# The output projection of a hybrid decoder layer by Strassen's seven products, with the combinations of weights and of the second half's input kept at the source's place in each engine's order

## The chip, the cores and the metric

The kernel runs on one core of one Trainium2 chip. Its time is the device time of one execution in microseconds; a run's time is the median of several executions where more than one is given. The engines are TensorE (PE, with its weight loads apart as PEld), VectorE (DVE), ScalarE (ACT), GpSimd (POOL) and SyncE, whose queue (SP) issues every DMA of this kernel.

## What is computed

One step of a Hymba-style layer: an RMS norm of the input, one input projection to all heads' queries, keys, values and gates, three kinds of recurrent heads (6 mLSTM heads "A", 6 gated-delta-rule heads "B", 4 HGRN2 heads "C", each 128 wide), a norm and a gate for each head, the output projection, the residual, a final norm. The width is 2048; there are 1024 prompt tokens, 16 meta tokens ahead of them, and 8 x 8 sample tokens. All is fp32. The end of it, which the change is about, is in the reference

```python
h = _rmsnorm(x, norm_w)
proj = jnp.einsum('bld,de->ble', h, w_in)
...
hcat = jnp.concatenate([ha, hb, hc], axis=2)
hcat = hcat * lax.rsqrt(jnp.mean(hcat * hcat, axis=-1, keepdims=True) + EPS)
y = hcat.reshape(bsz, L, MIX) * out_norm_w.astype(f32) * jax.nn.silu(z.astype(f32))
out = jnp.einsum('ble,ed->bld', y.astype(x.dtype), w_out)
return x + out, ...
...
y_prompt = _rmsnorm(xp[:, N_META:], final_norm_w)
```

so `out` is a product of 1024 x 2048 (and 64 x 2048 for the samples) by 2048 x 2048.

## The kernel before

The prompt is worked off in two halves of 512 tokens; the first half also holds the meta and the sample tokens. Every fp32 product is made of three fp32r products: each operand is split into a part `hi` and a rest `lo`, and hi·hi, hi·lo and lo·hi are added up. Weights come as pieces of 128x512: `feed_raw` loads one (tile `wraw`, four buffers), `feed_split` lets ACT cast it to `whi` and VectorE subtract to get `wlo` (four buffers each), and `feed_ahead` keeps the splits three pieces and the loads seven pieces ahead of the piece that TensorE is at. There are 720 pieces, 144 of them for the output projection.

For each half the heads are projected in the order of `ORDER` (C0 B0 A0 B1 A1 C1 B2 A2, then B3 A3 C2 B4 A4 B5 A5 C3); in the second half a piece is 12 matmuls of 128x512 (matmuls into `acc`). Between the matmuls the program weaves the heads' own work, as generators in four queues: `scan` (the recurrence), `fin` (`finish`: the head's norm, a turn through DRAM, the gate, the split into hi and lo, the store to `y_dram`), `post`, and `bg` (background: the preparation of the second half's input `prep_B`, norm states). A model clock (`Clock`) sets when a step is due, `Weave.pump` places due steps, and `drain` places all that is left of a stream. Behind that a scheduler may still move instructions within each engine's order, as far as their dependencies and its own estimate of their times allow. Each engine, and SP's queue, then works its instructions off in order.

A B head's scan (`gdn_scan`) solves a triangular system: `pkk` and `pqk` (matmuls of keys with keys and with queries) are scaled into `Ball`, its diagonal blocks make a turn through DRAM (`db`, `Bb`), VectorE substitutes in thirty small steps (`Yt`, `Yc`), transposes into `X`, and TensorE goes on with `pz` and `pyy`.

The output projection (1754 on) runs over `OUT_UNITS`: for the first half four groups of 512 columns with the half's four prompt tiles and the sample tile, for the second half the same without samples, the last group split in two. A unit takes 16 pieces (`o_raw`, one for each head of 128 rows), each with three matmuls for each prompt tile and two for the sample tile, into `oacc`. Then the tile of x is loaded and added, squared and summed, multiplied by the final norm's weights on POOL, and `final_norm` scales and stores the rows (tiles `res`, `oscr`, `fr`).

## Time and profile before

| | |
|---|---|
| median of three runs | 2505.61 us (2505.42 to 2511.15) |
| the profiled execution | 2506.0 us |
| its span | 2504.3 us, mean granted TensorE clock 0.990 |
| PE busy | 2442.1 us (98%) |
| VectorE, ACT, POOL busy | 1425.5, 991.2, 554.8 us |
| DMA | 350.82 MB, mean 140 GB/s |
| first and last output matmul | 2102.1 and 2493.5 us |

The span is the time between the first and the last instruction of the profiled execution. Busy times are sums over instructions, and since matmuls are pipelined and their ends modelled, a busy PE is not PE at its peak. L137 is the line of the helper that issues every engine instruction, so groups are told apart by their tiles.

### The profile page before, as it was taken

The numbers are of one execution on the slowest core, as the hardware profiler recorded it, in microseconds if no ns is written. First come the engines' busy times: TensorE is split into PE (matmuls) and PEld (weight loads), VectorE is DVE, ScalarE is ACT, GpSimd is POOL, SyncE is SP. The second block draws the span as 40 slices with busy tenths as digits, with TensorE's granted clock in tenths as the row PEclk, the third lists the DMA queues.
The fourth block names the chain that finished last, engine by engine and source line by source line (L and its number), as shares of the span: only waits on it lengthen the run. The fifth ranks groups of instructions, "written<-read, shape, count | busy, mean of one in ns | idle before, by whom it ended". The sixth has DMA issues, their size and how long they took to land.

```text
span 2504.3 us, 43941 instructions
## 1 busy us (share of the span) xinstructions
PE 2442.1 (98%) x16032; PEld 2184.5 (87%) x16032; DVE 1425.5 (57%) x3080; ACT 991.2 (40%) x2430; POOL 554.8 (22%) x743
## 2 busy tenths in 40 slices
PE   6999999999999999999999999999999999999998
PEld 5898999999999999999787888888888888888886
DVE  7775655765656655556864556554654545323435
ACT  5643434443435333333642434333443334222324
POOL 5331212420313312113320113110320102211201
PEclk9999999999999999999999999999999999999999
DMA  5656665655645454447554455454554558636735
GB/s 129 152 140 147 147 146 133 162 131 130 158 99 138 99 131 118 118 119 203 132 132 115 120 123 136 122 130 101 138 127 114 129 123 257 183 84 200 254 97 185
DMA packets 681045, 350.82 MB, mean 140 GB/s; under 512 B 260004, under 2 KB 622076, under 8 KB 680828
## 3 DMA queue, kind: packets, MB, share of 16 engines
q1 hardware_dynamic: 680828, 348.01, 54.3%
q8 instruction: 126, 2.06, 0.4%
q14 instruction: 91, 0.75, 0.1%
HBM read 285.71 MB, written 62.19 MB: 139 GB/s over the span
## 4 chain that ended last, share of the span: by engine, by line
PE 80%; issue 5%; DVE 5%; DMA 4%; ACT 2%; POOL 2%; SPq 1%; POOLq 0%; DVEq 0%; ACTq 0%
PE acc L137 59%; PE oacc L137 9%; PE pa L137 1%; DVE wlo L137 1%; PE po L137 1%; PE nd L137 1%; PE pz L137 1%; PE pyy L137 1%; DMA wraw<-in_w_in_dram 1%; POOL res L137 1%; PE pu L137 1%; DMA px<-in_x_prompt_dram 1%; ACT whi L137 1%; PE poh L137 1%; PE pw L137 1%
## 5 line engine op out<-in xcount | busy, mean ns | idle before, releaser
L137 DVE TENSOR_TENSOR wlo<-wraw,whi 128x512 fp32r<-128x512 f32 x720 | 525.6, 734 | 569.6 <-ACT whi L137 552.1
L137 PE MATMUL acc<-hA,whi 128*128 128x288 f32 (+1 forms) x4544 | 826.2, 304 | 11.3 <-ACT whi L137 6.4
L137 ACT CAST whi<-wraw 128x512 fp32r<-128x512 f32 x720 | 441.9, 618 | 929.1 <-PE acc L137 641.2
L137 PE MATMUL acc<-hB,whi 128*128 128x512 f32 x2272 | 722.2, 400 | 4.3 <-ACT whi L137 2.1
L137 PEld LDWEIGHTS acc<-hA,whi 128*128 128x128 f32 x4544 | 679.6, 191 | 18.2 <-ACT whi L137 8.1
L137 PE MATMUL acc<-hA,wlo 128*128 128x288 f32 x2240 | 489.7, 299 | 1.6 <-DVE wlo L137 1.6
L137 PEld LDWEIGHTS acc<-hB,whi 128*128 128x128 f32 x2272 | 413.6, 189 | 86.2 <-ACT whi L137 2.7
L137 PE MATMUL acc<-hB,wlo 128*128 128x512 f32 x1120 | 441.1, 394 | 2.6 <-DVE wlo L137 2.6
L137 PEld LDWEIGHTS acc<-hA,wlo 128*128 128x128 f32 x2240 | 367.7, 190 | 2.7 <-DVE wlo L137 2.6
L137 PE MATMUL oacc<-whi,y 128*128 128x512 f32 x1088 | 343.4, 390 | 1.1 <-ACT whi L137 1.1
L137 PEld LDWEIGHTS acc<-hB,wlo 128*128 128x128 f32 x1120 | 211.0, 188 | 52.0 <-DVE wlo L137 6.8
L137 PEld LDWEIGHTS oacc<-whi,y 128*128 128x128 f32 x1088 | 204.2, 188 | 44.5 <-ACT whi L137 2.4
L137 PE MATMUL oacc<-wlo,y 128*128 128x512 f32 x576 | 224.8, 390 | 1.2 <-DVE wlo L137 1.2
L137 PEld LDWEIGHTS oacc<-wlo,y 128*128 128x128 f32 x576 | 108.1, 188 | 25.2 <-DVE wlo L137 3.1
L137 POOL TENSOR_TENSOR res<-res,fnw 128x512 f32<-128x512 f32 (+1 forms) x34 | 54.3, 1627 | 255.4 <-ACT oscr L137 255.4
L137 POOL TENSOR_TENSOR y<-y,zs 128x592 fp32r<-128x592 f32 (+1 forms) x32 | 46.0, 1437 | 171.4 <-ACT zs L137 106.7
L137 POOL TENSOR_TENSOR qd<-qT,emb 128x512 f32<-128x512 f32 x12 | 17.7, 1479 | 230.3 <-PE po L137 230.3
L137 DVE TENSOR_TENSOR Yt<-Yc,Bb 128x60 f32<-128x60 f32 (+8 forms) x180 | 37.6, 209 | 43.9 <-DMA Bb<-db 39.0
L137 POOL TENSOR_TENSOR hr<-hr,halfneg 128x4 f32<-128x4 f32 (+1 forms) x48 | 44.1, 919 | 61.1 <-DVE hr L137 58.4
L137 POOL TENSOR_TENSOR nrm<-nrm,halfneg 128x10 f32<-128x10 f32 x12 | 23.5, 1960 | 138.9 <-DVE nrm L137 138.9
L137 POOL TENSOR_TENSOR X<-Ex,hk 128x256 f32<-128x256 f32 (+1 forms) x40 | 39.1, 978 | 63.2 <-PE pa L137 41.8
L137 ACT ACTIVATE Wt<-pw,nrm 128x128 f32<-128x128 f32 (+1 forms) x54 | 19.8, 367 | 78.1 <-PE pw L137 78.1
(416 smaller groups left out, 2766.7 us busy)
## 6 DMA issues: line engine op xcount, KB each, us to landing
wraw<-in_w_in_dram SPq DMA_DIRECT2D x564, 256.0 KB
wraw<-in_w_out_dram SPq DMA_DIRECT2D x144, 256.0 KB
y<-y SPq DMA_DIRECT2D x16, 576.0 KB
px<-in_x_prompt_dram SPq DMA_DIRECT2D x32, 256.0 KB
yd<-y SPq DMA_DIRECT2D x128, 64.0 KB
out_dram<-sst SPq DMA_DIRECT2D x16, 512.0 KB
s<-yd SPq DMA_DIRECT2D x32, 256.0 KB
y<-zs SPq DMA_DIRECT2D x32, 256.0 KB
```

Source lines behind the costliest of these rows:

```text
L137: return f(out, *a, **k)
```

## The change

The product is cut into 2 x 2 x 2 blocks: token halves, heads in two sets (`K1`, the first eight of `ORDER`, and `K2`, the other eight), and column halves. With A the gated heads' output and B the weights, seven block products take the place of eight. They use combinations of A's blocks, S1 to S4, and of B's, T1 to T4; A12, A21 and so on are never multiplied alone except where the scheme has them. The products run in seven phases over two buffers of y in turn; a phase has two parts `j` of 512 columns. The sample tokens' product isn't changed in its number of matmuls, and is done beside the phases that use the plain weights.

Beside the seven products it changes:

- `combine_weights`, a background stream of the second half: 16 times four loads of 128x512 weights, four POOL subtractions, four stores (`w_comb`). The 64 products' pieces then load from there (`c_raw`). The output projection has 152 pieces.
- `finish` of the first half also stores y whole (`y_whole`) and its POOL subtraction waits for that store, since it writes over y. In the second half a head of K1 makes S3 of y and the first half's y (one POOL step), a head of K2 makes S1, S2, S4 and A22 (three POOL steps); each combination is cast by ACT, subtracted by VectorE (by POOL before) and stored in two parts (`y_comb`).
- `load_y` loads the combinations for a phase and drains those finishes first whose results it needs.
- Partial sums (`t1`, `q`) stay in SBUF; ACT, VectorE and POOL move and add them between phases. x is loaded and added late.
- `prep_B` and `combine_weights` are pinned: their instructions keep the source's place in each engine's order (`tc.keep_in_program_order`), DMAs included.

The core of the diff:

```diff
+K1, K2 = HEADS[:NH // 2], HEADS[NH // 2:]
+LAST_UNITS = [(0, range(4)), (1, range(2)), (1, range(2, 4))]
...
+    def DMA(*a):
+        ins = nc.sync.dma_start(*a)
+        if ck.pin:
+            ck.pin(ins)
+        return ins
...
+    for j in range(2):
+        pieces += out_pieces(j, K1, j)
+    for j in range(2):
+        for a, b in zip(out_pieces(j, K2, j), out_pieces(j, K1, j + 2)):
+            pieces += [a, b]
+    for j in range(2):
+        for kk, b in enumerate(out_pieces(j, K2, j + 2)):
+            pieces += [(c_raw, "T2", j, kk), b]
+    for j in range(2):
+        pieces += [(c_raw, "T1", j, kk) for kk in range(NK // 2)]
+    for j in range(2):
+        pieces += out_pieces(j, K2, j + 2)
+    for j in range(2):
+        pieces += [(c_raw, "T3", j, kk) for kk in range(NK // 2)]
+    for j, _ in LAST_UNITS:
+        pieces += [(c_raw, "T4", j, kk) for kk in range(NK // 2)]
...
     def finish(half, head, outs, ssq, scale, zs):
...
+        if not half.first:
+            DMA(ya, y_whole[0][K1[kk]])
+            if not upper:
+                DMA(yb, y_whole[1][kk])
+                DMA(yc, y_whole[0][head])
...
+        if half.first:
+            S.copy(yhi[:, 0:W], y[:, 0:W])
+            ck.last += 1.0
+            yield
+            DMA(y_whole[0][head], y[:, 0:HALF])
+            ck.last = ck.t["T"] + 2.0
+            yield
+            G.tensor_tensor(ylo[:, 0:W], y[:, 0:W], yhi[:, 0:W], op=ALU.subtract)
...
+        def parts(src, hi, name):
+            S.copy(hi, src)
+            ck.sync()
+            V.tensor_tensor(src.bitcast(F32R), src, hi, op=ALU.subtract)
+            d = y_comb[name][kk].bitcast(F32)
...
+        G.tensor_tensor(yb, yb, y, op=ALU.add)
+        yield
+        yield from parts(y, yhi, "A22")
+        G.tensor_tensor(ya, yb, ya, op=ALU.subtract)
+        yield
+        yield from parts(yb, spare, "S1")
+        G.tensor_tensor(yc, yc, ya, op=ALU.subtract)
+        yield
+        yield from parts(ya, yhi, "S2")
+        yield
+        yield from parts(yc, spare, "S4")
...
+    def load_y(u, n, src):
+        if isinstance(src, str):
+            weave.drain(*(fins[1, h] for kk in (2 * n, 2 * n + 1) for h in (K1[kk], K2[kk])))
...
+    def combine_weights():
+        for j in range(2):
+            for kk in range(NK // 2):
+                b11, b12, b21 = (sp.tile([P, 512], F32, tag="px", name="px", bufs=3) for _ in range(3))
+                b22 = sp.tile([P, 512], F32, tag="pxs", name="pxs", bufs=1)
+                for t, heads, cg in ((b11, K1, j), (b12, K1, j + 2), (b22, K2, j + 2), (b21, K2, j)):
+                    DMA(t, i["w_out"][0, P * heads[kk]:P * (heads[kk] + 1), 512 * cg:512 * (cg + 1)])
+                for dst, a, b in ((b11, b12, b11), (b12, b22, b12), (b22, b22, b11), (b21, b21, b22)):
+                    ck.last = ck.t["T"] + 7.0
+                    yield
+                    G.tensor_tensor(dst, a, b, op=ALU.subtract)
+                ck.last = ck.t["T"] + 4.0
+                yield
+                for n, t in (("T1", b11), ("T3", b12), ("T2", b22), ("T4", b21)):
+                    DMA(w_comb[n][NK // 2 * j + kk], t)
...
+            weave.add("bg", combine_weights(), pin=tc.keep_in_program_order)
...
-                weave.add("bg", prep_B())
+                weave.add("bg", prep_B(), pin=tc.keep_in_program_order)
...
+    def phase(u, j, accs, tiles, own=None, other=None, each=None):
+        for kk in range(NK // 2):
+            whi, wlo = next_piece()
+            for n in tiles:
+                yh, yl = (y_block(u, kk, n, part) for part in (0, 1))
+                T.matmul(accs[n], yh, whi, start=kk == 0, stop=False)
+                T.matmul(accs[n], yh, wlo, start=False, stop=False)
+                T.matmul(accs[n], yl, whi, start=False, stop=kk == NK // 2 - 1)
...
+    for j, tiles in LAST_UNITS:
+        accs = banks(tiles)
+        phase(0, j, accs, tiles)
+        weave.drain_queue("post")
+        late = tiles[-1] == NC - 1 and j == 1
```

How the instructions move is seen at three places. First TensorE's order at head B4 of the second half, before (`acc` is the projection, `hB` the normed input, the rest the solver's tiles named above):

```order
L137 MATMUL pkk<-Ck 128x128 x4
L137 MATMUL acc<-hB_14743,whi 128x512
L137 MATMUL acc<-hB_14744,whi 128x512
L137 MATMUL acc<-hB_14743,wlo 128x512
...
L137 MATMUL pqk<-Cq,Ck 128x128 x4
...
L137 MATMUL pvb<-ident,Cv 128x128 x4
...
L137 MATMUL pz<-X_21883,Ball 32x32 x16
```

and in the change:

```order
L138 MATMUL acc<-hB_14984,wlo 128x512
L138 MATMUL pkk<-Ck 128x128 x4
L138 MATMUL pqk<-Cq,Ck 128x128 x4
L138 MATMUL pvb<-ident,Cv 128x128 x4
L138 MATMUL pz<-X_22217,Ball 32x32 x16
L138 MATMUL acc<-hB_14767,whi 128x512
L138 MATMUL acc<-hB_14768,whi 128x512
```

Before, 9, 6 and 78 projection matmuls stand in the three gaps; now there are none between `pkk` and `pz`.

Second POOL's order where the second half begins (`px` and `pxs` are the weights being combined; `sst`, `state_C` and `hr` belong to the scan and the finish of the first half's last head):

```order
L138 TENSOR_TENSOR pxs<-pxs,px 128x512
L138 TENSOR_TENSOR px<-px,pxs 128x512
L138 TENSOR_TENSOR sst<-sst,eP 128x8x128
L138 COPY state_C_772<-s_15301 128x128
L138 TENSOR_TENSOR hr<-hr,halfneg 80x1
L138 TENSOR_TENSOR hr<-hr,halfneg 128x4
L138 TENSOR_TENSOR px<-px 128x512
L138 TENSOR_TENSOR px<-pxs,px 128x512
```

The rows on `px` and `pxs` are new; they stand ahead of and between the steps of that scan.

Third ACT's order in the first half, where before the squares of the second half's input (`pxs<-px`) stand among the gate scan's steps:

```order
L137 ACTIVATE Lr<-Lr 128x592
L137 CAST whi<-wraw 128x512
L137 ACTIVATE pxs,bss<-px 128x512
L137 ACTIVATE gt_970<-pre 128x592
L137 ACTIVATE pxs,bss<-px 128x512
L137 ACT_TABLE_LOAD
```

and in the change among a head's finish some 90 pieces on:

```order
L138 CAST whi<-wraw 128x512
L138 ACTIVATE pxs,bss<-px 128x512
L138 CAST zs<-y 128x592
L138 ACTIVATE t_5332<-pot 80x128
L138 CAST whi<-wraw 128x512
```

All sixteen squares have moved so.

More of the change, by code (lines that the diff above doesn't have):

```diff
@@ L855, in finish @@
         turn_in(hrs[-1], d)
+        if not half.first:
+            DMA(ya, y_whole[0][K1[kk]])
+            if not upper:
+                DMA(yb, y_whole[1][kk])
+                DMA(yc, y_whole[0][head])
         ck.last = ck.t["T"] + 5.0
@@ L1727, in final_norm @@
                 yield
+            free.extend(res.pop((n, cg)) for cg in order)
     def norm_states():
```

349 lines of the change are left out of this document (247 added, 102 removed).

## The prediction

> **What bounds the kernel now.** I read the page's first and fourth parts, then windows by stage, then the chain, then the timelines round one head.
>
> ```profile
> span 2504.3 us, 43941 instructions
> PE 2442.1 (98%) x16032; PEld 2184.5 (87%) x16032; DVE 1425.5 (57%) x3080; ACT 991.2 (40%) x2430; POOL 554.8 (22%) x743
> PE 80%; issue 5%; DVE 5%; DMA 4%; ACT 2%; POOL 2%; SPq 1%; POOLq 0%; DVEq 0%; ACTq 0%
> PE acc L137 59%; PE oacc L137 9%; PE pa L137 1%; DVE wlo L137 1%; PE po L137 1%; PE nd L137 1%; PE pz L137 1%; PE pyy L137 1%; DMA wraw<-in_w_in_dram 1%; POOL res L137 1%; PE pu L137 1%; DMA px<-in_x_prompt_dram 1%; ACT whi L137 1%; PE poh L137 1%; PE pw L137 1%
> ```
>
> TensorE is busy for 2442.1 of 2504.3 us, and on the chain that ends last the projection's and the output projection's matmuls stand first. The windows say where TensorE is not full.
>
> ```profile
> 60.00:140.00 80.00, 71.12 (x496) 68.17 (x495) 52.85 (x120) 52.04 (x110) 25.91 (x50) 0.98 0.68 165
> ...
> 1150.00:1250.00 100.00, 92.51 (x519) 76.16 (x518) 70.52 (x128) 50.71 (x103) 30.27 (x33) 0.98 0.66 180
> 1250.00:2102.00 852.00, 849.28 (x4799) 703.75 (x4798) 468.11 (x996) 320.81 (x765) 144.66 (x165) 1.00 0.52 132
> ...
> 2200.00:2300.00 100.00, 100.00 (x443) 82.81 (x442) 30.46 (x43) 26.79 (x54) 15.09 (x10) 1.00 0.43 129
> 2300.00:2400.00 100.00, 99.61 (x439) 81.93 (x438) 38.64 (x71) 31.32 (x60) 18.87 (x14) 1.00 0.68 221
> 2400.00:2504.00 104.00, 92.28 (x401) 74.51 (x399) 48.32 (x78) 38.31 (x74) 18.23 (x14) 0.97 0.50 150
> ```
>
> After a window's length the columns give the busy time of PE, PEld, DVE, ACT and POOL, then the granted clock, the share of the DMA engines and their rate. From 1250 to 2102 us PE lacks 2.7 us of 852, and in the output projection it lacks nothing from 2200 to 2300 us. Idle time stands at the start (60 to 140 us: 8.9 us) and between the halves (1150 to 1250 us: 7.5 us). So a matmul that is taken out of the output projection shortens the span by its own time, provided that the stages around it stay full; and anything that empties TensorE for a while in a stage that is full now is paid in full.
>
> **The change part by part.** *Matmuls.* The chain gives the pace of the stage, and the groups its number.
>
> ```profile
> 2163.80 149.21 PE oacc L137 x658
> ...
> 2478.12 5.50 DMA wraw<-in_w_out_dram
> ...
> 2491.09 2.12 PE oacc L137 x8
> ```
>
> and of the groups
>
> ```profile
> L137 PE MATMUL oacc<-whi,y 128*128 128x512 f32 x1088 | 343.4, 390 | 1.1 <-ACT whi L137 1.1
> L137 PE MATMUL oacc<-wlo,y 128*128 128x512 f32 x576 | 224.8, 390 | 1.2 <-DVE wlo L137 1.2
> ```
>
> 658 matmuls of 128x512 in 149.21 us are 0.2268 us each. The stage has 1088 + 576 = 1664; of these 1536 are the prompt's. Strassen's scheme makes 7 products of 3 x 4 x 16 = 192, so 1344, and with the 128 for the samples 1472: 192 fewer, 192 x 0.2268 = **-43.5 us**. This term is the surest one, for both units before and phases after are the same 128x512 matmuls.
>
> *The last unit.* The chain holds a wait for weights that were issued late (2478.12), and its last matmuls end at 2493.2, 11.1 us ahead of the end. Of the last 104 us PE is busy for 92.28, so beside that tail 0.6 us are idle, and the clock's 0.97 costs up to 3.1. In the changed order all weights stand ahead of the outputs on SP's queue. I take **-1 us**, with bounds of -3 and +1 (a longer tail).
>
> *Head B4 of the second half.* This is the largest price, and it comes from a place that the diff does not show. Each GDN head runs pkk, then the decay matrix Ball, a round trip to DRAM (db, Bb), thirty small VectorE steps (Yt, Yc) and a transpose into X, before pz can start. Before, 93 projection matmuls stand between pkk and pz; in the changed order none do, only pqk and pvb. In every other B head of the second half the cover is as before, or within 12 matmuls of it. Here are PE, then DVE, SP's queue and POOL at that head before (start, us, instruction).
>
> ```profile
> 1882.22 1.06 PE L137 MATMUL pkk<-Ck 128*128 128x128 f32 x8
> ...
> 1885.19 1.06 PE L137 MATMUL pqk<-Cq,Ck 128*128 128x128 f32 x8
> ...
> 1887.46 0.60 PE L137 MATMUL pvb<-ident,Cv 128*128 128x128 f32 x4
> ...
> 1905.71 0.89 PE L137 MATMUL pz<-X,Ball 32*32 32x32 f32 x32
> ```
>
> ```profile
> 1883.45 1.12 DVE L137 SCALAR_TENSOR_TENSOR Ball<-pkk,nrm,Ball 128x128 f32<-128x128 f32 x4
> ...
> 1896.02 0.22 DVE L137 TENSOR_TENSOR Yt<-Yc,Bb 128x60 f32<-128x60 f32 x1 [4.69 <-DMA Bb<-db]
> ...
> 1900.84 0.19 DVE L137 TENSOR_TENSOR Yt<-Yc,Bb 128x28 f32<-128x28 f32 x1
> 1901.07 0.60 DVE L137 TENSOR_TENSOR Yc<-Yc,Yt 128x28 f32<-128x28 f32 x1
> ...
> 1902.88 0.69 DVE L137 TENSOR_TENSOR wlo<-wraw,whi 128x512 fp32r<-128x512 f32 x1
> ...
> 1905.04 0.31 DVE L137 STREAM_TRANSPOSE X<-Y 128x128 f32<-128x128 f32 x1
> ```
>
> ```profile
> 1884.59 6.05 SPq L1207 DMA_DIRECT2D db<-Ball  x8
> ...
> 1892.04 1.92 SPq L1213 DMA_DIRECT2D Bb<-db  x3
> ```
>
> ```profile
> 1900.99 0.63 POOL L137 TENSOR_SCALAR_AFFINE_SELECT bb<-bb 128x512 f32<-128x512 f32 x1 [5.23 <-DMA bb<-rows]
> ```
>
> And what PE did with its projection matmuls in that stretch:
>
> ```profile
> 1882.20:1905.40 23.20, 21.71 (x94) 17.24 (x93) 0.00 (x0) 1.17 (x2) 1.00 0.46 118
> ```
>
> From pkk (1882.22) to pz (1905.71) are 23.5 us, of which 21.7 were covered by 94 projection matmuls. In the changed order DVE has no weight split between Yt and X, which saves three times some 0.6 us (the one at 1902.88 is the last). So the chain takes about 21 us; pkk, pqk and pvb fill 1.06 + 1.06 + 0.60 = 2.7 of them, and PE stands for **+18.4 us**. The work that covered it isn't lost, but it comes afterwards (123 projection matmuls ahead of the next pst, where 30 stood before), where nothing was missing. Lower bound: +15, if the round trip is faster on a quieter queue (issue of the eight db stores took 6.05 us of it); upper bound: +23, if Ball waits behind the finish of head C2, whose last VectorE step and two weight splits (0.69 us each) stand ahead of it. Then the clock:
>
> ```profile
> 100.00:104.00 4.00, 2.15 (x12) 1.84 (x11) 1.82 (x4) 3.76 (x9) 0.94 (x1) 0.82 0.86 244
> 104.00:108.00 4.00, 4.00 (x25) 4.00 (x25) 3.91 (x13) 3.48 (x8) 0.00 (x0) 0.75 0.29 75
> ```
>
> In 100 to 108 us PE stood for 1.85 us of 4 and the granted clock was 0.82 and 0.75. I charge the lost shares, 4 x 0.18 + 4 x 0.25 = **+1.7 us**. The Trainium skill (TensorE: Matmul & The Clock Gate, Part 1: The HAM clock gate) says that after an idle window of about 3.4 us the array runs at half clock until it has been busy for about as long; by that the loss would be half of 3.4, an estimate of 1.7 us as well, but paid for each such gap. The row agrees in its lowered clock, not in a value of one half.
>
> *The start.* The input preparation of the second half (`prep_B`) is now kept in its place; before, the scheduler had drawn its loads and squares into 70 to 131 us, where these stood on the chain:
>
> ```profile
> 91.37 8.44 DMA px<-in_x_prompt_dram
> ...
> 125.11 4.60 DMA px<-in_x_prompt_dram
> ...
> 131.75 3.19 DMA pnw<-in_norm_w_dram
> ```
>
> and the squares of it:
>
> ```profile
> L137 ACT ACTIVATE pxs<-px x16: 613/633/642, 69.6 to 131.0; 128x512 f32<-128x512 f32 x16
> ```
>
> They are 16.2 us of chain, in a window in which PE lacked 8.9 us. The squares now stand 300 us later, where PE has work. I take **-6 us** of those 8.9: the bounds are -12 (all of the window's loss with its lowered clock, 0.98 of 80 us, and some more) and 0 (the gate scan's own waits remain).
>
> *Between the halves.* `combine_weights` starts there. Its first four loads (1 MB) and first three POOL subtractions stand ahead of weights and of the scan's POOL steps, in a window that already lost 7.5 us with DMA at 0.66. 1 MB at the rate of that window, 180 GB/s, is 5.8 us; three POOL steps by the row below are 4.7. I take **+5 us**, bounds 0 and +9.
>
> *The finishes.* Each head of the second half now forms its combinations. For the eight heads of K2 that is three POOL steps, four casts, and VectorE subtractions, in order ahead of the next weights' splits.
>
> ```profile
> L137 DVE TENSOR_TENSOR wlo<-wraw,whi 128x512 fp32r<-128x512 f32 x720 | 525.6, 734 | 569.6 <-ACT whi L137 552.1
> L137 ACT CAST whi<-wraw 128x512 fp32r<-128x512 f32 x720 | 441.9, 618 | 929.1 <-PE acc L137 641.2
> L137 POOL TENSOR_TENSOR res<-res,fnw 128x512 f32<-128x512 f32 x30 | 46.4, 1568 | 255.4 <-ACT oscr L137 255.4
> L137 POOL TENSOR_TENSOR y<-y,zs 128x512 fp32r<-128x512 f32 x16 | 21.0, 1310 | 124.3 <-ACT zs L137 76.9 <-DMA wraw<-in_w_in_dram 45.4 <-issue 2.0
> ```
>
> A finish that is drained at once holds VectorE from y to the last part: per round one POOL step of 1.31, a cast of 0.62 and a subtraction of 0.7, 2.6 us, three times and once more a POOL step of `combine_weights` of 1.57 between them: 8 to 11 us. The splits run three pieces ahead, 3 x 12 x 0.2268 = 8.2 us of cover. So a head costs 0 to 3 us. Most heads have their finish spread out by the planner; I count two such, and in the first phases, where every second piece of weights feeds two sample matmuls only (16 matmuls for two pieces, 5.4 us of cover for three), the scan of C3, whose steps have less cover (2 matmuls where 14 stood): **+6 us**, bounds 0 and +20.
>
> *The first half.* The moved `prep_B` changes the order there: at one B head three steps of the solver lose the 6 to 12 matmuls between them, at another one step, and the last C head two. Each is a hop from PE to DVE and back: 0.17 us from pkk's end to Ball, a small step of some 0.3, and 0.36 from X's end to pz, so 0.8 us, six times at most: **+4 us**, bounds 0 and +8.
>
> *DMA in the phases.* A phase of 192 matmuls lasts 43.5 us. The fullest, the sixth, loads 4.2 MB of weights, 4.2 of y, 2.1 of x and stores 4.2 MB: 14.7 MB, 338 GB/s. Before:
>
> ```profile
> 2340.00:2360.00 20.00, 20.00 (x90) 16.57 (x89) 6.36 (x10) 5.16 (x9) 0.00 (x0) 1.00 0.99 353
> ```
>
> 353 GB/s with PE at 20.00 of 20 us. So I cost it at **0**; it is hidden by weights being issued seven pieces ahead (19 us), and if that cover is gone, 14.7 MB at the 244 GB/s that 100 to 104 us show take 60 us: +17 at most.
>
> *The sum*, against the profiled execution's 2506.0 us (its span of 2504.3 and 1.7 around it; the runs' median is 2505.61, the same within 0.02%): -43.5 - 1 + 18.4 + 1.7 - 6 + 5 + 6 + 4 = -15.4, so about **2490 us**.
>
> **The rivals.** *The small prices aren't paid.* If start and last unit give what I took and the finishes, the boundary and the first half cost nothing, 2506 - 43.5 - 1 + 18.4 + 1.7 - 6 = 2476; with the start's full 12, 2469. For it: PE's 849 of 852 us in the second half, through heads whose scans are no lighter. Against it: every finish stands in the same in-order queues as the splits.
>
> *The combinations starve the splits.* All eight K2 finishes are drained ahead of splits and each overruns the cover by its 3 us (24), the sixth phase adds 17, the boundary its 9: 2490 - 6 + 24 + 17 + 4 = 2529. It decides from the point at which VectorE's work between two splits passes 8.2 us at every K2 head. For it: POOL gets 64 steps of 1.57 more (100 us). Against: the planner spaces them by its own clock, and in the order only about two heads show it.
>
> *POOL blocks VectorE.* In the timeline above a Yc step took 0.60 us where the one before it (1900.84) took 0.19, exactly while POOL ran its 0.63 us on bb (1900.99). If each of 64 + 24 new POOL steps delays a VectorE step by its own length, 1.4 us on average, that is 120 us on VectorE, which is busy 468 of 852 us: it is hidden but for the finishes and solvers, where I charge half a POOL step per head, 16 x 0.8 = +13: 2503. The Trainium skill (SBUF — State Buffer, on the shared port pair) has such a rule: a VectorE instruction with two inputs in SBUF and a GpSimd instruction that reads SBUF exclude each other for a whole instruction; the one row agrees.
>
> *It doesn't do what it says.* The order shows 1472 matmuls, so this is left out.
>
> **How the numbers follow.** Forecast 0.45, small prices unpaid 0.27, POOL blocks 0.15, starved 0.13. Range 2465 to 2510: from the second case's low end to beyond the fourth's, leaving out the starved one and a little below. A difference of 0.3% (7.5 us) is about what can be told from no change: faster is under 2498, slower over 2513. Faster holds most of the forecast (0.40), all of the second (0.27) and a little of the third (0.04): 0.71. Same: 0.05 + 0.10 = 0.15. Slower: 0.13 and 0.01: 0.14.
>
> **What would show it.** 1472 output matmuls in place of 1664, at 0.227 us each. At the last but one pkk: a PE gap of 15 to 23 us before pz, released by DVE's X, with a lowered clock behind it. Between 60 and 140 us: PE busy for more than 71.12 us. Between the halves: more idle than 7.5 us. Idle before PE by whi and wlo in the second half: some 6 us. If pz finds X ready, or if PE waits for weights by tens of us in the phases, I am wrong.

## The result and the profile after

The changed kernel takes 2639.62 us (median of four runs, 2637.47 to 2641.8), the kernel before beside it 2505.97: a ratio of 1.0531, 95% interval 1.0514 to 1.0548. It is 134 us slower, where it was forecast to be 15 us faster.

The page of the changed kernel, its span, busy times, TensorE's granted clock in 40 slices, and the end of the chain of waits:

```profile
span 2639.2 us, 44255 instructions
PE 2443.9 (93%) x15840; PEld 2179.7 (83%) x15840; DVE 1550.5 (59%) x3160; ACT 1016.5 (39%) x2476; POOL 701.1 (27%) x855
PEclk9999999999799999999997999999997999999999
PE 8%; POOL 1%; issue 1%; DMA 1%; DVE 1%; ACT 0%; SPq 0%; POOLq 0%; DVEq 0%; ACTq 0%
```

192 matmuls are gone (15840 in place of 16032), yet PE's busy time is as before: its matmuls are slower where the clock is down (133 us of the busy time lie at a clock of 0.50, 42 us before). The chain now reaches back only through the last phases, so it says nothing of the middle. The windows do; the columns are those of the prediction, the fourth row is the stage from the first to the last output matmul:

```profile
60.00:140.00 80.00, 74.93 (x543) 72.70 (x543) 60.95 (x129) 42.94 (x79) 29.71 (x55) 1.00 0.48 111
600.00:680.00 80.00, 54.42 (x401) 52.73 (x401) 35.59 (x76) 21.21 (x56) 5.39 (x13) 0.84 0.61 131
1150.00:1250.00 100.00, 97.72 (x701) 93.81 (x701) 58.38 (x130) 41.75 (x99) 26.46 (x30) 0.98 0.67 181
2247.00:2628.00 381.00, 356.60 (x1578) 290.07 (x1576) 207.69 (x301) 143.01 (x281) 125.51 (x97) 0.97 0.71 228
```

The start is fuller than before (74.93 for 71.12 of 80). A stretch that the prediction does not mention, 600 to 680 us, has lost a third of its work. The output stage lacks 24 us of 381 and runs at 0.97.

A sharper reading lays the two traces side by side by work and not by time: the start of the n-th projection matmul after, minus its start before. I call it the drift. It grows only where the change loses time.

| place (time before, us) | drift after, us | gained or lost since the row above |
|---|---|---|
| 147, start of the first half's stream | -7.4 | -7.4 |
| 1141, end of the first half | +63.0 | +70.4 |
| 1296, past the boundary | +72.0 | +9.0 |
| 1868, ahead of head B4 | +110.0 | +38.0 |
| 1954, behind head B4 | +141.6 | +31.6 |
| 2102, first output matmul | +145.3 | +3.7 |
| 2493, last output matmul | +134.4 | -10.9 |

With the tail (11.3 us after the last output matmul, 10.8 before) that is the 134.9 us between the two spans.

**The first half.** What TensorE waited for, by the view of waits (total, times, longest), has one wait that the kernel before does not have at all:

```profile
PE pz L138 <- DVE Yc L138: 45.3, 4, 28.2
PE acc L138 <- ACT whi L138: 32.7, 14, 7.6
PE pum L138 <- DMA s<-vT: 20.8, 1, 20.8
PE acc L138 <- DVE wlo L138: 15.1, 13, 2.9
PE oacc L138 <- ACT whi L138: 14.6, 4, 9.0
```

`pum` belongs to a head's scan. It waits for a turn through DRAM (`s<-vT`) which SP issues. SP's queue, then DVE, ACT and PE in that stretch (start, us, instruction, idle before it):

```profile
644.48 0.55 SPq L207 DMA_DIRECT2D sst<-in_state_mlstm_C_dram  x1
662.56 1.96 SPq L207 DMA_DIRECT2D hbhi<-px  x4
...
670.58 0.45 SPq L207 DMA_DIRECT2D s<-vT  x1
```

```profile
656.08 0.28 DVE L138 TENSOR_SCALAR Ck<-U,params 128x64 f32<-128x64 f32 x1 [1.30 <-ACT U L138]
...
661.18 0.70 DVE L138 STREAM_TRANSPOSE xT<-px 128x512 f32<-128x512 f32 x1
```

```profile
661.92 0.62 ACT L138 CAST px<-xT 128x512 fp32r<-128x512 f32 x1 [1.46 <-DVE xT L138]
```

```profile
655.20 0.43 PE L138 MATMUL acc<-hA,wlo 128*128 128x288 f32 x2
676.43 2.06 PE L138 MATMUL pum<-s,kwall 128*128 128x129 f32 x8 [20.80 <-DMA s<-vT]
```

`hbhi<-px` stores a result of `prep_B`. It needs ACT's cast at 661.92, which needs DVE's transpose `xT` at 661.18, and that stands on DVE behind the convolution steps `Ck`, which need `U` from PE's accumulators. So SP stands for 17 us (645.0 to 662.56) with the weights, and the scan's turn through DRAM, behind it. When it is free, PE has nothing left. A background step had become part of the foreground of four engines. This gap is one of several: between 560 and 800 us SP waits six times, 43.8 us in all, for such a cast (`px` of ACT), and 56 of the 70.4 us come between the matmuls that stood at 575 and 740 us before (the drift goes from +0.9 to +56.9).

**Head B4 of the second half.** PE, then DVE and POOL:

```profile
1992.22 1.06 PE L138 MATMUL pkk<-Ck 128*128 128x128 f32 x8
...
1994.01 0.60 PE L138 MATMUL pvb<-ident,Cv 128*128 128x128 f32 x4
2022.83 1.32 PE L138 MATMUL pz<-X,Ball 32*32 32x32 f32 x32 [28.22 <-DVE Yc L138]
```

```profile
1990.99 1.77 DVE L138 TENSOR_TENSOR yb<-yb,yc 128x512 fp32r<-128x512 f32 x1 [1.19 <-POOL ya L138]
1992.69 1.75 DVE L138 TENSOR_TENSOR wlo<-wraw,whi 128x512 fp32r<-128x512 f32 x1
...
1997.75 0.68 DVE L138 TENSOR_TENSOR wlo<-wraw,whi 128x512 fp32r<-128x512 f32 x1
...
2000.16 1.12 DVE L138 SCALAR_TENSOR_TENSOR Ball<-pkk,nrm,Ball 128x128 f32<-128x128 f32 x4
```

```profile
1990.92 1.29 POOL L138 TENSOR_TENSOR px<-px,pxs 128x512 f32<-128x512 f32 x1
1992.18 1.72 POOL L138 TENSOR_TENSOR yc<-yc,ya 128x512 f32<-128x512 f32 x1
```

The gap stands where it was foreseen, but it is 28.2 us and not 18.4. From Ball to X the solver takes 22.5 us (21.9 before). Ball itself starts 6.9 us after pkk's end, where 0.2 us passed before: a finish's combinations and the weights' splits stand ahead of it on DVE, and so does a step of its own factor `nrm`, for which DVE waits 2.07 us for POOL. And two of these steps take 1.77 and 1.75 us while POOL runs its 128x512 steps; the same step takes 0.68 when POOL is idle (1997.75). Behind the gap the clock:

```profile
2029.00:2030.00 1.00, 1.00 (x4) 0.80 (x3) 0.00 (x0) 0.00 (x0) 0.00 (x0) 0.50 0.00 0
...
2031.00:2032.00 1.00, 1.00 (x18) 0.89 (x18) 0.40 (x1) 0.53 (x2) 0.00 (x0) 0.76 0.00 0
2032.00:2034.00 2.00, 2.00 (x31) 1.42 (x31) 0.35 (x2) 0.35 (x2) 0.00 (x0) 1.00 0.20 40
```

**The output projection.** At a phase's end POOL adds the partial sums, ACT squares the result, and the casts of the next weights are queued behind the squares:

```profile
2354.47 3.54 POOL L138 TENSOR_TENSOR res<-res,t 128x512 f32<-128x512 f32 x2
```

```profile
2356.25 0.63 ACT L138 ACTIVATE oscr<-res 128x512 f32<-128x512 f32 x1 [1.70 <-POOL res L138]
2358.04 0.63 ACT L138 ACTIVATE oscr<-res 128x512 f32<-128x512 f32 x1 [1.07 <-POOL res L138]
...
2359.29 1.14 ACT L138 CAST whi<-wraw 128x512 fp32r<-128x512 f32 x2
```

```profile
2359.95 0.50 PE L138 MATMUL oacc<-whi,y 128*128 128x512 f32 x1 [1.16 <-ACT whi L138]
```

By the view of waits PE stands 14.6 us for such casts in this stage. The longest of them, 9.0 us, is not at a phase's end. It stands in the first phase, where the scan of C3 and the finish of a head before it are still worked off. SP's queue, ACT and PE there:

```profile
2278.34 1.93 SPq L207 DMA_DIRECT2D wraw<-in_w_out_dram  x4
```

```profile
2282.32 2.67 ACT L138 CAST whi<-wraw 128x512 fp32r<-128x512 f32 x4 [5.97 <-DMA wraw<-in_w_out_dram]
```

```profile
2282.99 0.80 PE L138 MATMUL oacc<-whi,y 128*128 128x512 f32 x1 [8.97 <-ACT whi L138]
```

For the 20 us ahead of 2278.34 SP issues no piece of weights; it stands 11.1 us for the first of the finish's stores, and the other stores and the scan's turn through DRAM follow.

So three suspects came out of the traces: `prep_B` in its fixed place (first half), POOL's steps of 128x512 beside VectorE (second half and phases), and the cover that is gone at B4. The experiments take them one by one.

### The profile page after: what moved, and what is told of

Same layout as the page of the kernel before. It is cut to its first block, busy times and chain, and to the rows that moved or that the text cites. A ratio compares the mean times of both kernels' runs of the same rounds, so it can differ in the third digit from the quotient of the medians.

```text
span 2639.2 us, 44255 instructions
## 1 busy us (share of the span) xinstructions
PE 2443.9 (93%) x15840; PEld 2179.7 (83%) x15840; DVE 1550.5 (59%) x3160; ACT 1016.5 (39%) x2476; POOL 701.1 (27%) x855
## 5 line engine op out<-in xcount | busy, mean ns | idle before, releaser
L138 DVE TENSOR_TENSOR wlo<-wraw,whi 128x512 fp32r<-128x512 f32 x728 | 562.7, 782 | 454.1 <-ACT whi L138 419.9
L138 PE MATMUL acc<-hB,whi 128*128 128x512 f32 x2272 | 735.8, 406 | 15.3 <-ACT whi L138 13.0
L138 PEld LDWEIGHTS acc<-hA,whi 128*128 128x128 f32 x4544 | 684.5, 192 | 32.0 <-ACT whi L138 22.1
L138 PEld LDWEIGHTS acc<-hB,whi 128*128 128x128 f32 x2272 | 421.4, 192 | 99.6 <-ACT whi L138 14.5
L138 PE MATMUL oacc<-whi,y 128*128 128x512 f32 x928 | 299.8, 397 | 14.7 <-ACT whi L138 14.6
L138 PEld LDWEIGHTS oacc<-whi,y 128*128 128x128 f32 x928 | 177.9, 192 | 54.9 <-ACT whi L138 17.5
L138 PE MATMUL oacc<-wlo,y 128*128 128x512 f32 x480 | 191.4, 399 | 9.2 <-DVE wlo L138 9.2
L138 PEld LDWEIGHTS oacc<-wlo,y 128*128 128x128 f32 x480 | 91.9, 191 | 31.5 <-DVE wlo L138 12.4
L138 PE MATMUL pz<-X,Ball 32*32 32x32 f32 x576 | 21.4, 213 | 62.7 <-DVE Yc L138 45.3
L138 PEld LDWEIGHTS pz<-X,Ball 32*32 32x32 f32 x576 | 18.7, 125 | 70.4 <-issue 51.8
L138 POOL TENSOR_TENSOR res<-res,fnw 128x512 f32<-128x512 f32 (+1 forms) x30 | 42.9, 1451 | 64.6 <-ACT oscr L138 64.6
```

The costliest lines, as they stand in the source:

```text
L138: ins = f(out, *a, **k)
```

## The experiments

The runs are numbered by their labels (8 and 10 are not in use). Times are medians; ratios are against the kernel before, run beside them (2503.3 to 2505.5 us). Runs 5 to 7 leave combinations out and so give another `y_prompt`; the others compute what the changed kernel computes.

### 1 to 4: the pinning

```diff
 # 1: the changed kernel
-                weave.add("bg", prep_B(), pin=tc.keep_in_program_order)
+                weave.add("bg", prep_B())
 # 2: the changed kernel, pinned engine steps, free DMAs
     def DMA(*a):
-        ins = nc.sync.dma_start(*a)
-        if ck.pin:
-            ck.pin(ins)
-        return ins
+        return nc.sync.dma_start(*a)
 # 3: as 1, and
-            weave.add("bg", combine_weights(), pin=tc.keep_in_program_order)
+            weave.add("bg", combine_weights())
 # 4: the kernel before, with the change's code for pinning, and
-                weave.add("bg", prep_B())
+                weave.add("bg", prep_B(), pin=tc.keep_in_program_order)
```

> The changed kernel with prep_B alone left to the scheduler as before (combine_weights stays pinned). In the changed kernel's trace the first half ends 62.8 us behind the kernel before, and SP stood up to 17.4 us at a time at the pinned stores hbhi. Theory A (the pinned stores and loads of prep_B hold SP's queue, and weights and the scans' turns through DRAM wait behind them): the first half loses nothing but the start's 7.4 us come back, so 2640 less 63, about 2577, 2565 to 2585. Theory B (the first half loses by the added stores of y whole, for which POOL's subtraction in each finish has to wait): the loss stays, 2630 to 2645.

Measured: 2580.85 us (2578.99 to 2582.9), ratio 1.0307 [1.0292, 1.0323], 58.8 us less than the changed kernel, as theory A has it. The stretch that had lost a third of its work is full again:

```profile
600.00:680.00 80.00, 80.00 (x624) 79.29 (x625) 51.73 (x116) 32.67 (x89) 20.55 (x31) 1.00 0.64 154
```

The drift at the end of the first half falls from +63.0 to +8.9. At the start it rises from -7.4 to -2.0: the relief of the start does come from the pinning, 5.4 us of it, and is paid for ten times over later.

> The changed kernel with the engines' instructions of prep_B and combine_weights pinned as in the change, but their DMAs left to the scheduler. Theory A in its strict form (only where the DMAs stand on SP's queue counts): 2565 to 2580, as without the pin of prep_B, less the start's 7 us. Rival A' (the pinned engine steps themselves come late, and whatever needs their results waits wherever its DMA stands): little changes, 2625 to 2645. Theory B: little changes as well.

Measured: 2640.98 us (2633.13 to 2642.51), ratio 1.0541 [1.052, 1.0562], no change. That the DMAs' own pin is what costs falls: the free stores stand at the same place in SP's queue, SP still waits 17.5 us for ACT's `px` ahead of 664.93, and the gap at `pum` is 20.9 us. ACT's and DVE's pinned steps come late whether the store is pinned or not. (Theory B allows for no change as well, but run 1 has ruled it out as the main cause.)

> The changed kernel with neither stream pinned. By theory A for the first half it is at least as fast as e1_prep_free there. For the second half: if the pinned stores and POOL steps of combine_weights are what makes the rest of the loss (82 us from the halves' boundary to the output projection), it comes to 2500 to 2540; if the loss there is the finishes' own work and head B4's missing cover, it stays near e1_prep_free, 2565 to 2590.

Measured: 2603.3 us (2599.16 to 2611.94), ratio 1.0401 [1.0377, 1.0425], 22 us more than with only `prep_B` free, and in neither of the expected ranges. The pin on `combine_weights` is worth keeping: without it its loads and subtractions are drawn into the first half, where the drift reaches +59.1 by 1141 us (+8.9 with it), while the second half then loses less.

> The kernel before with one part of the change alone: prep_B pinned, its DMAs included; no Strassen products, no combinations. Theory A: the first half loses here as in the change, 2506 + 55 to 65, so 2560 to 2572. Theory B: only the start's relief remains, 2495 to 2502.

Measured: 2549.39 us (2546.84 to 2552.91), ratio 1.0186 [1.0168, 1.0205], 46 us more than the kernel before, short of the 2560 to 2572 expected. One argument in the old kernel, with nothing of Strassen in it, costs most of the 58.8 us, at the same place:

```profile
PE pum L138 <- DMA s<-vT: 17.3, 1, 17.3
```

So the pinning's part of the first half's loss is shown twice, by undoing it and by doing it alone.

### 5 to 7: which part of the combinations

```diff
 # 5: as 1; the pieces T1 to T4 load plain weights
-        DMA(raw, w_comb[name][NK // 2 * j + kk])
+        heads, cg = {"T1": (K1, j), "T2": (K2, j + 2), "T3": (K1, j + 2), "T4": (K2, j)}[name]
+        DMA(raw, i["w_out"][0, P * heads[kk]:P * (heads[kk] + 1), 512 * cg:512 * (cg + 1)])
...
-            weave.add("bg", combine_weights(), pin=tc.keep_in_program_order)
 # 6: as 1; the second half's finish splits y alone and stores it as S1 to S4 and A22
-        G.tensor_tensor(yb, yb, y, op=ALU.add)
-        yield
-        yield from parts(y, yhi, "A22")
...
+        S.copy(yhi, y)
+        yield
+        V.tensor_tensor(y.bitcast(F32R), y, yhi, op=ALU.subtract)
+        yield
+        for name in (("S3",) if upper else ("A22", "S1", "S2", "S4")):
+            d = y_comb[name][kk].bitcast(F32)
+            DMA(d[:, 0:HALF], yhi.bitcast(F32))
+            DMA(d[:, HALF:], y)
 # 7: both
```

> As e1_prep_free (2581), but the stream combine_weights is left out: no loads, POOL steps and stores of T1 to T4; the products that use them read plain blocks of the output weights instead, so y_prompt is another sum. From the halves' boundary to the output projection e1_prep_free loses 76 us. Theory C (the weights' combinations: POOL's 64 steps, their DMAs, and what they hold up): 40 to 60 of them go, 2520 to 2540. Theory F (the finishes' combinations, queued ahead of weights' splits and of the solver's Ball, and head B4's missing cover): 5 to 20 go, 2560 to 2576.

Measured: 2551.1 us (2542.96 to 2555.21), ratio 1.018 [1.0155, 1.0206], 30 us less than run 1, between the two expected ranges. The drift ahead of B4 falls from +53.1 to +29.1; the step at B4 (25.4 for 29.2 us) and the output stage (380.9 us) stay nearly as they were.

> As e1_prep_free (2581), but the second half's finishes form no combinations: no loads of y whole, no POOL steps, one cast and one VectorE subtraction in each head; all stores stay and write y's two parts, so y_prompt is another sum. In its order 93 projection matmuls stand between pkk and pz of head B4 again. Theory F: B4's 29 us, the 12 us ahead of it and most of the start of the output projection's 12 go, 2520 to 2540. Theory C: only B4's 29 go, 2548 to 2560.

Measured: 2529.83 us (2528.03 to 2538.01), ratio 1.0106 [1.0082, 1.013], 51 us less than run 1, as theory F has it. In its order 93 projection matmuls stand again between pkk and pz of B4, and the drift over B4 is +5.2 (+29.2 in run 1). POOL's steps and the missing cover go together here; runs 9 and 11 take them apart.

> As e1_prep_free without both (no combine_weights, plain finishes in the second half), so that Strassen's phases with their moves stand alone. By the sum of matmuls (192 x 0.2268 = 43.5) and with 9 us lost in the first half: 2504 - 43.5 + 9 + about 20 that the phases lose at their ends = 2490, 2480 to 2500. If the phases lose their 32 us whatever runs before them, 2500; if the loss of the second half has yet another cause, above 2520.

Measured: 2501.86 us (2497.21 to 2516.36), ratio 0.9993 [0.998, 1.0006], 79 us less than run 1. The two savings add up (30 + 51 = 81). But with every combination gone, the 43.5 us of matmuls taken out still don't show: its output stage takes 376.7 us for 391.2, where 391.2 - 43.5 = 347.7 would be without loss. (That is the profiled execution, at 2516.36 us the slowest of ten, so some us of it may be its own.) So a third loss sits in the phases, and none of runs 5 to 7 takes most of it away.

### 9: POOL's steps on VectorE

Run 1, with the combinations and the phases' sums moved from POOL to VectorE, eight lines of this kind:

```diff
-        G.tensor_tensor(ya, yb, ya, op=ALU.subtract)
+        V.tensor_tensor(ya, yb, ya, op=ALU.subtract)
...
-                    G.tensor_tensor(dst, a, b, op=ALU.subtract)
+                    V.tensor_tensor(dst, a, b, op=ALU.subtract)
...
-            G.tensor_tensor(t, t, q[j, n], op=ALU.add)
+            V.tensor_tensor(t, t, q[j, n], op=ALU.add)
```

> As e1_prep_free (2581), with every new 128x512 step of POOL done by VectorE (the 64 of combine_weights, those of the second half's finishes, the sums in the output projection's phases; POOL keeps the multiplication by the final norm's weights). VectorE gets some 130 steps of 0.7 us more. Theory P (the new POOL steps block VectorE's two-input steps, which took 1.77 us in place of 0.69 beside them, and hold what is queued on POOL): the second half loses 25 to 45 us less and the phases 8 to 15, 2525 to 2550. Rival (VectorE's own queue is what is full): no gain or a loss, 2575 to 2600. B4's missing cover is in this order too and stays in both.

Measured: 2541.42 us (2536.66 to 2545.21), ratio 1.0145 [1.0124, 1.0166], 39.4 us less than run 1. More work on the busier engine, and faster. The output stage falls from 379.7 to 359.9 us, 19.8 us where 8 to 15 were expected, and the second half loses 18.4 us less where 25 to 45 were expected; the sum was right, its parts weren't. The gap at B4 stays:

```profile
1945.27 1.32 PE L138 MATMUL pz<-X,Ball 32*32 32x32 f32 x32 [20.67 <-DVE Yc L138]
```

It is 20.7 us now, near the 18.4 forecast: what is left when Ball starts 0.9 us after pkk's end and not 6.9.

### 11 to 14: the cover, the store, and POOL once more

```diff
 # 11: as 9; a drain ahead of a head ends once the finish has formed y
-        while any(not s.done for s in streams):
+        while any(not s.done and not getattr(s, 'freed', False) for s in streams):
...
         y, yhi = y[:, 0:HALF], yhi[:, 0:HALF]
+        fins[half.index, head].freed = True
...
-            weave.drain(*(fins[1, h] for kk in (2 * n, 2 * n + 1) for h in (K1[kk], K2[kk])))
+            for h in [h for kk in (2 * n, 2 * n + 1) for h in (K1[kk], K2[kk])]:
+                fins[1, h].freed = False
+                weave.drain(fins[1, h])
 # 12: as 11; in the first half lo is written beside y, not over it
-            G.tensor_tensor(ylo[:, 0:W], y[:, 0:W], yhi[:, 0:W], op=ALU.subtract)
+            low = hrs[-1].rearrange("p c t -> p (c t)").bitcast(F32R)
+            G.tensor_tensor(low, y[:, 0:HALF], yhi[:, 0:HALF], op=ALU.subtract)
+            G.tensor_tensor(ylo[:, HALF:W], y[:, HALF:W], yhi[:, HALF:W], op=ALU.subtract)
 # 13: as 12; the final norm's weights by VectorE, together with the row's scale
-        if not late:
+        if not late and n >= 7:
             G.tensor_tensor(t[:cnt], t[:cnt], fnw[cg][:cnt], op=ALU.mult)
...
-                if x == 3 and late:
+                if n < 7 or x == 3 and late:
                     V.scalar_tensor_tensor(t[:cnt], t[:cnt], r, fnw[cg][:cnt], op0=ALU.mult, op1=ALU.mult)
 # 14: as 12, with the eight lines of 9 on POOL again
```

By its code, the planner is the cause of the missing cover. When a head starts, the finishes of earlier heads are drained, and the model clock jumps ahead to each step's due time. The longer finish makes it jump over the time in which pieces would have been placed; the solver's steps are then all due at once, and stand in the order with no projection between them. Run 11 changes the drain alone.

> As e9_vector_combines (2541.42 us), but a finish no longer has to be drained through its combinations before the next head but one starts: a drain ends once the gated y is formed, and the combinations go on beside the next heads; load_y still drains them before they are read. Nothing is left out. In the order 90 projection matmuls stand again between pkk and pz of head B4 of the second half (0 in e9_vector_combines), and 93 in every other B head there. Theory C (the price of B4 is the missing cover; at e9's trace the drift grows by 33 to 36 us from 1913 to 1985 us, of which some 6 are given back): 2541 - 27 = about 2514, 2506 to 2522, with a stall of under 4 us before that pz and no clock of 0.50 behind it. Rival W (what holds pz is VectorE's work of the combinations, which is still there and now stands elsewhere): the time is given back at the splits, over 2530.

Measured: 2498.26 us (2489.85 to 2506.97), ratio 0.997 [0.9948, 0.9993], 43.2 us less than run 9, and beyond the low end of what was expected. PE over B4's solver, from pkk at 1906.86:

```profile
1904.00:1928.00 24.00, 24.00 (x118) 20.12 (x117) 14.88 (x45) 7.78 (x16) 0.30 (x1) 1.00 0.75 229
```

The second half loses 5.1 us in all (drift +18.7 to +23.8), where run 9 lost 57.0 (+9.9 to +66.9): 26.6 of that at B4, the rest at the finishes and at three other heads that had 79, 81 and 81 matmuls of cover and have 93 again. The profiled run is 8.8 us further behind at the end of the first half than run 9, with the same covers there: 2.0 of it at the start, the rest at two B heads, where the clock stays at 0.50 for 17.1 and 10.2 us (13.7 and 6.8 in run 9). Why it does so is open.

> As e11_cover_back, and in the first half's finish the rest of y (the part lo) is written to the turned tile and not over y, so POOL's subtraction doesn't wait for the store of the whole y, and one POOL step on the samples is added. Nothing is left out. In the order the covers of the first half's B heads are those of the kernel before again (150, 162, 156, 162, 156, 162). Theory F (the 10 us that each of the runs without the pinned prep_B loses between 900 and 1000 us of the first half come from that wait and its due times): 8 to 10 us less than e11_cover_back, about 2505. Rival (they come from the stores themselves, 4 MB more on SP's queue): the same within 3 us.

Measured: 2481.31 us (2477.76 to 2497.13), ratio 0.9916 [0.9889, 0.9943], 17.0 us less than run 11. The drift at the end of the first half is -0.6 (run 11: +18.7, run 9: +9.9). So the wait for the store of y, with its due times, cost about 10 us by run 9's drift and 19 by run 11's, which holds the 8.8 us left open above; 8 to 10 were expected. Two things changed at once here, the wait and the order that the planner makes of it, and they aren't told apart.

> As e12_no_store_wait, and the final norm's weights are multiplied in by VectorE with the row's scale in one step, for all tiles but the last two, in place of a POOL step of 1.57 us each at the phases' ends and a scaling on VectorE or ACT. Nothing is left out. Theory P (POOL's 128x512 steps beside VectorE's two-input steps cost in the phases): the output projection, 360 us in e9_vector_combines, falls to 352 to 356, and the time by 4 to 8 us against e12_no_store_wait, which would put it at or just under the kernel before. Rival (what is left there is the order of ACT's casts behind its squares): the same within 2 us.

Measured: 2478.23 us (2472.2 to 2487.0), ratio 0.9896 [0.9861, 0.9931]. The 3.1 us to run 12 are less than the two intervals can tell apart; the output stage, 356.8 to 353.8 us, points the same way. This is the fastest version, 27 us under the kernel before:

```profile
span 2470.5 us, 44204 instructions
PE 2399.4 (97%) x15840; PEld 2150.6 (87%) x15840; DVE 1550.9 (63%) x3295; ACT 1008.6 (41%) x2467; POOL 498.7 (20%) x715
...
1250.00:2102.00 852.00, 846.65 (x4796) 700.86 (x4795) 532.46 (x1114) 329.72 (x786) 132.37 (x153) 1.00 0.67 185
```

From 1250 to 2102 us PE works 846.65 of 852 us at a clock of 1.00, with all combinations in place. VectorE is busy for 532 us where it was 468 before, and PE waits for it 5.4 us in all.

> As e12_no_store_wait, but all the 128x512 steps that the change adds (those of the finishes, of combine_weights and the sums of the phases) stand on POOL again, as in the changed kernel; so this is the changed kernel with prep_B free, the cover of the solvers back and no wait for the store of y. Nothing is left out. Theory P (POOL's steps cost by themselves, by their length and by doubling VectorE's steps beside them): the 39.5 us between e1_prep_free and e9_vector_combines come back, 2481 + 39 = about 2520, with 20 us of it in the output projection. Rival I (POOL costs mostly where the cover was gone, so that the second half now hides it): only the output projection loses, 2481 + 20 = about 2501 or less.

Measured: 2534.38 us (2524.66 to 2538.91), ratio 1.0111 [1.0081, 1.014], 53.1 us more than run 12. The output stage loses 20.7 us of it (377.5 for 356.8), and the drift at the first output matmul is +44.1 for +5.2. That is 14 us above what theory P expected. So POOL's steps are not only dear where the cover is gone: the second half pays for them with its cover in place. What PE waits for in VectorE's splits goes from 2.7 to 12.6 us there, in the output stage from 2.0 to 9.2. VectorE's groups show these splits. The split of the weights in the changed kernel, in run 12 and in run 14 (count, busy us, mean ns):

```profile
L138 DVE TENSOR_TENSOR wlo<-wraw,whi 128x512 fp32r<-128x512 f32 x728 | 562.7, 782 | 454.1 <-ACT whi L138 419.9
```

```profile
L138 DVE TENSOR_TENSOR wlo<-wraw,whi 128x512 fp32r<-128x512 f32 x728 | 533.5, 739 | 428.9 <-ACT whi L138 397.3 <-DMA wraw<-in_w_in_dram 5.8 <-PE oacc L138 5.4
```

```profile
L138 DVE TENSOR_TENSOR wlo<-wraw,whi 128x512 fp32r<-128x512 f32 x728 | 560.6, 778 | 448.0 <-ACT whi L138 424.9 <-PE oacc L138 9.5 <-PE po L138 5.1
```

The mean goes from 739 to 778 ns; the kernel before had 734. The mean hides it, for the median is 691 ns in all of them and few splits are held up: over 1.6 us take 8 of 720 splits before, 41 of 728 in the changed kernel, 19 in run 12 and 38 in run 14, counted in the traces. Each of these overlaps a POOL step, and without one beside it no split takes over 0.73 us. Not told apart is how much of the 53 us comes from VectorE's longer steps and how much from POOL's own, of 1.3 us and more where VectorE takes 0.7, on whose results other engines wait.

Together, from the changed kernel to run 13: `prep_B` free -58.8, POOL's steps to VectorE -39.4, the cover back -43.2, the store's wait -17.0, the norm -3.1 (within the noise). That is 2639.62 to 2478.23.

## Why the prediction was wrong, step by step

**The start, -6: right.** The drift at 147 us is -7.4, 5.4 of it from the pinning by run 1. It is the one part of the first half that went as forecast.

**The first half, +4: wrong, by 66 us, the largest error.** The drift grows by 70.4 there. The step that failed is "the squares now stand 300 us later, where PE has work", and the sum of six hops of 0.8 us with it. I looked at what stood beside the moved steps in PE's order alone. But a step of `prep_B` is a chain over DVE, ACT, DVE and SP, and each link is queued behind foreground work and in front of other foreground work. I asked what is queued behind a wait on PE, and not on SP, where 17 us of waiting held back the weights. Runs 1 and 4 put the pinning at 59 and 46 us. The rest is some 9 us, which run 1 still loses by the end of the first half and run 12 doesn't: the store of y, which I had not priced, with its due times.

**The boundary, +5: right in kind.** It took 9.0, the upper bound. With `prep_B` free it is 10.4 in run 1 and 3.7 in run 9: most of it was POOL.

**The finishes, +6 (0 to 20): wrong.** Beside the boundary and B4 the second half lost 41.7 us. The step that failed is "So a head costs 0 to 3 us": it looked for the price at the weights' splits. There PE waits 9.4 us in all between 1368 and 1978 us, not far from the forecast. Of the 38.0 us lost ahead of B4, 13.4 and 10.6 are lost at two other B heads, B0 and B2, whose `pz` waits, and 12.1 behind a cast that comes late:

```profile
1408.58 1.35 PE L138 MATMUL pz<-X,Ball 32*32 32x32 f32 x32 [9.24 <-DVE X L138]
...
1711.94 1.35 PE L138 MATMUL pz<-X,Ball 32*32 32x32 f32 x32 [6.88 <-DVE X L138]
...
1913.91 1.22 PE L138 MATMUL acc<-hB,whi 128*128 128x512 f32 x2 [7.06 <-ACT whi L138]
```

Before, the first two waits are 2.3 and 0 us. Around the end of each of the three the clock is at 0.50, for 27.3, 13.7 and 6.8 us; the first:

```profile
1403.40:1430.70 27.30, 22.12 (x155) 16.25 (x156) 10.25 (x35) 2.12 (x5) 1.83 (x4) 0.50 0.41 104
```

The covers there are 75 and 81 matmuls (81 and 93 before), and from `pkk` to `pz` it is 28.6 and 27.7 us for 23.1 and 23.5. A round was priced at VectorE's usual durations, "a subtraction of 0.7". It is 1.7 beside POOL, and so are the splits between, ahead of the solver's steps; and a drained finish shortens the covers of the heads behind it. Run 11, without POOL's steps and with all covers at 90 or 93, loses 5.1 us in the whole second half.

**Head B4, +18.4 and the clock +1.7: the mechanism was right, its size too small.** The gap was 28.2, the drift 31.6. From Ball to X the sum had about 20 us, 21.9 less three splits; it took 22.5. The larger miss is that Ball starts 6.9 us after pkk and not 0.2. The upper bound of 23 named that cause and took each step at 0.69. The clock stood at 0.50 from 2022.8 to about 2031, so some 4 us in place of 1.7. In run 9, without POOL's steps, the gap was 20.7. Run 11 shows that the price was the cover's: with it back, the drift doesn't grow there (+24.0 to +22.1).

**The matmuls, -43.5: right in the count and the pace, but the stage gained only 10.9.** 1472 output matmuls ran. The step that failed is the cost of 0 for the phases: it was argued for DMA's rate, and for the rate it holds, with PE full at 262 GB/s (this window of the changed kernel):

```profile
2400.00:2500.00 100.00, 100.00 (x441) 82.55 (x440) 47.13 (x74) 31.90 (x55) 14.15 (x11) 1.00 0.79 262
```

The cover by weights issued ahead, on which the 0 also rested, failed once, in the first phase, for the 9.0 us shown above. What I had not costed at all are the phases' ends, where sums on POOL stand ahead of squares and casts on ACT. With POOL's steps on VectorE (run 9 against run 1) the stage is 19.8 us shorter, with them back (run 14 against run 12) 20.7 longer. Run 13 brings it to 353.8 us, 37.4 less than before and 6.1 short of the forecast.

**The last unit, -1:** the tail grew by 0.5, within the bounds.

**The rivals.** "POOL blocks VectorE" was held at 0.15 and priced at +13, half a POOL step for each head. Its mechanism was the truth of the second half, at 39 us with the covers broken (run 9 against run 1) and 53 with them whole (run 14 against run 12). The Trainium skill (SBUF — State Buffer, on the shared port pair) has the rule for it: of a VectorE step with two inputs in SBUF and a GpSimd step that reads SBUF, the one that starts later is blocked until the other has ended. The rows agree: 1.77 us is close to a step of 0.69 behind most of POOL's 1.29. That the price was so small came from spreading it evenly over the heads, where the loss stands at few places: B0, B2, B4, the phases' ends. That the combinations starve the splits (2529) was right in direction; none of the rivals held the pinned `prep_B`, since I took the move of a background step for cheap.

## What to carry to other kernels

An instruction that is fixed in its place is a promise on every in-order queue that it touches: follow its whole chain, DMAs and all, and ask on each queue what stands behind it, not only what PE does meanwhile. An idle GpSimd is no free room for 128x512 sums beside a VectorE that works on two inputs; here the same sums were 39 and 53 us cheaper on the busier engine (runs 9 and 14). And where a planner's clock sets the order, a longer background job can take away the cover of a quite different one: count the matmuls between a solver's start and its first use in the order, for each head.

## What the runs showed of the hardware that I had not expected

VectorE's two-input steps of 128x512 take 1.75 to 1.77 us beside a POOL step of the same size, 0.68 to 0.69 alone.

The clock came back at different speeds. Behind the 20.8 us gap of the first half:

```profile
676.40:678.00 1.60, 1.57 (x7) 1.60 (x8) 0.33 (x2) 0.95 (x2) 0.00 (x0) 0.50 1.19 310
680.00:682.00 2.00, 2.00 (x24) 1.80 (x19) 1.69 (x6) 0.88 (x2) 1.69 (x1) 1.00 0.92 218
```

and behind the gap at B4:

```profile
2023.00:2024.00 1.00, 1.00 (x32) 1.00 (x30) 0.00 (x0) 0.00 (x0) 0.00 (x0) 0.50 0.00 0
```

After the 20.8 us gap at 655 us it was at 1.00 from 680 us on, about 3.6 us after work began at 676.4; after the 28.2 us gap at B4 it stayed at 0.50 from 2022.8 to 2031 (the rows of B4 above give its end). The Trainium skill (TensorE: Matmul & The Clock Gate, Part 1: The HAM clock gate) says that the full clock comes after at least one busy window, about 3.4 us of sustained work; the first gap agrees, and the second took more than twice as long. What differs is that work of 32x32 stands between the projection's matmuls in the second. The traces of all fourteen kernels have nineteen gaps of over 8 us behind 150 us: ten end at `pz`, and the clock is full again 7.4 to 22.1 us after work begins; nine end at other work, and it takes 3.1 to 7.0 us. That points at the small matmuls, but no run changed them alone.
